# Zero rows of the last batch shared out by the engines' counted rows, the copies of the first two batches queued in another order, and one semaphore for the free transfers, in an argmax, gather and scatter kernel

## The chip, the core and the metric

The kernel runs on one core of one Trainium2 chip. The metric is device time in microseconds (us) of one execution. Executions of one kernel on one chip mostly agree within about 0.4%. The chips differ too: the kernel before took 857.7 us on one, 860.0 to 860.2 us on two others. So times are compared with the kernel before on the same chip in the same rounds.

## The reference

For each of 8 batches there are 2048 rows of 2048 scores, and 2048 value rows of 2560 float32 (10,240 bytes each). For each score row the reference finds the column of the largest score. It then adds that column's value row into the output at the same index, so an output row is its value row times the number of score rows that chose it.

```python
best_j = np.argmax(scores, axis=2)
gathered = values[b_idx, best_j, :].copy()
out = np.zeros_like(values)
np.add.at(out, (b_idx, best_j, slice(None)), gathered)
```

With the fixed inputs, of the 16,384 output rows 6,131 are chosen by nobody (they must be zero), 5,875 once (a copy of the value row) and 4,378 more than once (a scaled copy).

## The kernel before

(HBM stands for the memory of the source's DRAM tensors, the inputs and the output; its tiles are in SBUF, or in PSUM where their pool says so.) SyncE loads score tiles of 2 MB. VectorE finds each row's maximum and its index; TensorE adds one-hot matrices into a count for every column. From the counts VectorE makes index lists. GpSimd then issues indirect DMAs, 128 rows each: copies from HBM to HBM of the rows chosen once, zero rows from SBUF to HBM, and for the other rows a gather into SBUF (ScalarE scales them there) and a scatter. An index out of range skips its row: in the packet records it leaves a packet of 4 bytes, recorded as 9 ns, where a row that is moved is one of 10,240 bytes, 385 ns in the median. A copy needs only the counts, but a zero row or a gather needs the list, which is made later (cuts are marked):

```python
def value_steps(b, cnt_ps):
    # ... one_i: index of rows with count 1, out of range for the others
    first = NT if b == 0 else 4          # copies queued before the list exists (NT = 16)
    for t in range(first):
        copy_once(t)
    # ... ranks of the zero rows and of the others, by scans and two matmuls
    yield
    # ...
    oh = ohp.tile([P, 2 * NT, P], FP16)
    nc.vector.tensor_tensor(out=oh[:], in0=lo[:]..., in1=fill_f[:]..., op=ALU.is_equal)  # 4.4 us
    # ... matmuls that turn ranks into lists
    yield
    yield
    # ... zi, mi: the lists
    if b == 0:
        zeros()                          # 7 zero scatters
        for _ in range(10):
            yield
        gathers()                        # 5 gathers
    else:
        gathers()                        # each followed by one of the copies left over
        zeros()                          # likewise
    for k in range(MCAP):
        scatter(staged[k], mi[:, k:k + 1])
```

Each `yield` hands VectorE back to the scores of the next batch. For batch 0 the first four steps are taken at once, without pause. The transfers that nothing waits for (copies and zero rows) are "free": they increment `landed[b]`, one semaphore for each batch, and GpSimd waits for all eight at the end. `fill_f` decides on which partition of a list a rank falls; its order deals successive ranks out to the DMA engines in turn, if the map from partition to engine is the one that is read from the packets below.

## Time and profile before

| Kernel before | |
|---|---|
| median of 3 runs | 857.89 us (857.76 to 858.29) |
| span of the profiled run | 859.2 us |
| bytes moved by the DMA engines | 347.05 MB |
| rate in undisturbed slices | 427 GB/s |
| VectorE busy | 687.9 us, its last work at 708 us |
| last row packet ends | 847.4 us |

The page shows the span in 40 equal slices of 21.5 us, so slice 0 starts at 0 and slice 4 at 86 us. The first line is the busy share of the 16 DMA engines in tenths, the second what they moved.

```profile
DMA  9999899996999999999999999999999999999980
GB/s 378 427 427 427 289 390 428 419 413 248 428 419 426 427 426 429 426 429 424 427 426 428 425 427 428 429 426 425 428 424 420 424 426 413 425 425 421 425 370 35
DMA packets 47248, 347.05 MB, mean 404 GB/s; under 512 B 18278, under 2 KB 18278, under 8 KB 18278
```

The reader should see a kernel bound by its DMA engines: 427 GB/s nearly everywhere, and a few slices that fall short. Those are slices 4 and 5 (289 and 390), slice 9 (248) and the end (370 and 35). The windows view resolves them. Its columns are the stretch and its length, the busy time of each engine, TensorE's clock, the DMA engines' busy share, and GB/s.

```profile
core 0: us, PE busy (x) PEld busy (x) DVE busy (x) ACT busy (x) POOL busy (x), PEclk, DMA share, GB/s
86.00:116.00 30.00, 1.45 (x38) 1.40 (x38) 26.47 (x41) 0.00 (x0) 22.44 (x19) 1.00 0.89 308
186.00:208.00 22.00, 1.27 (x36) 1.19 (x36) 21.69 (x30) 0.00 (x0) 3.32 (x5) 1.00 0.65 240
830.00:838.00 8.00, 0.00 (x0) 0.00 (x0) 0.00 (x0) 0.00 (x0) 0.00 (x0) 1.00 0.64 269
838.00:848.00 10.00, 0.00 (x0) 0.00 (x0) 0.00 (x0) 0.00 (x0) 0.00 (x0) 1.00 0.17 69
848.00:859.10 11.10, 0.00 (x0) 0.00 (x0) 0.00 (x0) 0.00 (x0) 0.00 (x0) 1.00 0.00 0
```

From 830 us on no compute engine works; engines run out of rows one after the other (0.64, then 0.17 busy), and for the last 11 us no row moves. The timeline shows who should have fed slices 4 and 9. Its columns are start, duration, engine and line, operation, and in brackets the idle time before it and what ended it.

```profile
89.44 4.42 DVE L239 TENSOR_TENSOR oh<-lo,fill_f 128x4096 f16<-128x4096 uint32 x1
89.50 5.22 POOL L33 DMA_INDIRECT out_dram<-in_values_dram,ones_i  x1 [0.30 <-issue]
...
95.02 1.01 POOL L33 DMA_INDIRECT out_dram<-in_values_dram,ones_i  x1 [0.30 <-issue]
...
```

```profile
182.61 0.98 POOL L33 DMA_INDIRECT out_dram<-in_values_dram,ones_i  x1 [11.48 <-DVE m L214]
...
186.45 0.97 POOL L33 DMA_INDIRECT out_dram<-in_values_dram,ones_i  x1 [0.30 <-issue]
205.19 1.04 POOL L134 DMA_INDIRECT vbig<-in_values_dram,many_i  x1 [17.77 <-DVE empty L270]
```

In batch 0 one issue takes 5.22 us where the median of all 264 is 0.98 us. In batch 1 four copies are issued by 187.4 us, and then GpSimd waits 17.77 us for the list.

The *shortfall* of a stretch is its length less the time that the bytes moved in it would take at 427 GB/s, from the packet records, a packet's bytes spread over its duration. The *tail* is the time from an even end to the last row packet; the even end is 800 us plus a sixteenth of the time of all packets that start after 800 us. *After the last packet* is what remains of the span. In this trace the shortfall of 86 to 230 us is 18.9 us, the tail 10.2 us, and 11.7 us follow the last packet.

### The profile page before, as it was taken

To read this page: it belongs to the slowest core of one execution; us is meant where nothing else is said; L and a number is where in the kernel's file an instruction comes from. 1 tells how busy PE (TensorE), PEld (TensorE's weight loads), DVE (VectorE), ACT (ScalarE), POOL (GpSimd) and SP (SyncE) were. 2 spreads that over 40 slices of the span, in tenths; PEclk is the share of its full clock that TensorE was granted. 3 is DMA by queue.
4 is the path that set the end of the run, shared out by engine and by line. 5 is a ranking of instruction groups with operands and counts; after the bars stand their busy time and mean duration, and the time that the engine had idled before them with its cause. 6 is when DMAs were issued, how large, how long until landed. Compare 5 with 4: busy or idle time off the path is not lost.

```text
span 859.2 us, 2246 instructions
## 1 busy us (share of the span) xinstructions
PE 18.0 (2%) x400; PEld 17.0 (2%) x400; DVE 687.9 (80%) x741; ACT 103.2 (12%) x43; POOL 271.7 (32%) x275
## 2 busy tenths in 40 slices
PE   0000000000000000000000000000000000000000
PEld 0000000000000000000000000000000000000000
DVE  6999899999999999999999999999999980000000
ACT  2000000500320000220002300013100500500400
POOL 0000751213721027140056210451306715716500
DMA  9999899996999999999999999999999999999980
GB/s 378 427 427 427 289 390 428 419 413 248 428 419 426 427 426 429 426 429 424 427 426 428 425 427 428 429 426 425 428 424 420 424 426 413 425 425 421 425 370 35
DMA packets 47248, 347.05 MB, mean 404 GB/s; under 512 B 18278, under 2 KB 18278, under 8 KB 18278
## 3 DMA queue, kind: packets, MB, share of 16 engines
q0 software_dynamic: 38016, 212.67, 59.8%
q1 hardware_dynamic: 9216, 134.22, 37.1%
q14 instruction: 13, 0.11, 0.0%
q8 instruction: 3, 0.05, 0.0%
HBM read 354.42 MB, written 293.60 MB: 754 GB/s over the span
## 4 chain that ended last, share of the span: by engine, by line
DVE 69%; DMA 9%; POOL 7%; issue 5%; another core or an unknown queue 4%; PE 0%; POOLq 0%
DVE am L169 31%; DVE mx L168 29%; DMA out_dram<-vbig,many_i 8%; DVE oh L239 3%; POOL out_dram L33 3%; POOL out_dram L139 3%; DVE oh_lo L178 2%; POOL vbig L134 1%; DMA vbig<-in_scores_dram 1%; DVE lo L174 1%; DVE oh_hi L182 0%; DVE rz L247 0%; DVE hi L176 0%; DVE ez L243 0%
## 5 line engine op out<-in xcount | busy, mean ns | idle before, releaser
L169 DVE FIND_INDEX8 am<-mx,s_tile 128x8 uint32<-128x2048 f32 x116 | 265.1, 2285 | 0.0
L168 DVE MAX8 mx<-s_tile 128x8 f32<-128x2048 f32 x116 | 264.4, 2279 | 0.0
L280 ACT ACTIVATE vbig<-vbig,many_c 128x2560 f32<-128x2560 f32 x40 | 96.9, 2427 | 705.9 <-DMA vbig<-in_values_dram,many_i 703.1
L33 POOL DMA_INDIRECT out_dram<-in_values_dram,ones_i x128 | 130.1, 1016 | 155.3 <-DVE m L214 117.0
L134 POOL DMA_INDIRECT vbig<-in_values_dram,many_i x40 | 40.6, 1015 | 260.5 <-DMA out_dram<-vbig,many_i 198.1
L139 POOL DMA_INDIRECT out_dram<-vbig,many_i x40 | 41.4, 1035 | 105.8 <-ACT vbig L280 101.1
L139 POOL DMA_INDIRECT out_dram<-zrow,zero_i x56 | 58.3, 1042 | 17.1 <-issue 17.1
L239 DVE TENSOR_TENSOR oh<-lo,fill_f 128x4096 f16<-128x4096 uint32 x8 | 35.5, 4434 | 0.0
L168 DVE MAX8 mx<-vbig 128x8 f32<-128x2048 f32 x12 | 27.4, 2280 | 6.2 <-DMA vbig<-in_scores_dram 6.2
L169 DVE FIND_INDEX8 am<-mx,vbig 128x8 uint32<-128x2048 f32 x12 | 27.4, 2285 | 0.0
L178 DVE TENSOR_TENSOR oh_lo<-lo,lane_f 128x512 bf16<-128x512 uint32 x32 | 22.2, 695 | 0.3
L187 PE MATMUL cnt_ps<-oh_hi,oh_lo 128*128 128x16 bf16 x128 | 8.2, 174 | 571.2 <-DVE oh_hi L182 542.4
L187 PEld LDWEIGHTS <-oh_lo 128*128 128x128 bf16 x128 | 8.4, 105 | 570.9 <-DVE oh_lo L178 521.3
L169 DVE MATCH_VALUE_LOAD am<-mx,s_tile 128x8 f32 x116 | 10.7, 92 | 4.0
L174 DVE TENSOR_SCALAR lo<-am 128x4 uint32<-128x4 uint32 x32 | 6.1, 192 | 1.1
L182 DVE TENSOR_TENSOR oh_hi<-hi,lane_f 128x64 bf16<-128x64 uint32 x32 | 7.0, 218 | 0.0
L258 PE MATMUL m_ps<-rm,oh 128*128 128x16 f16 x128 | 4.7, 175 | 81.1 <-DVE rm L254 81.1
L176 DVE TENSOR_SCALAR hi<-am 128x4 uint32<-128x4 uint32 x32 | 6.1, 191 | 0.0
L258 PEld LDWEIGHTS <-oh 128*128 128x128 f16 x128 | 4.1, 105 | 81.6 <-DVE rm L254 74.8
L261 PE MATMUL z_ps<-rz,oh 128*128 128x16 f16 x128 | 4.6, 174 | 0.0
L261 PEld LDWEIGHTS <-oh 128*128 128x128 f16 x128 | 4.0, 104 | 0.0
L247 DVE TENSOR_TENSOR rz<-ez,row_f 128x256 f16<-128x256 f16 x8 | 3.4, 424 | 0.3
(52 smaller groups left out, 54.5 us busy)
## 6 DMA issues: line engine op xcount, KB each, us to landing
s_tile<-in_scores_dram SPq DMA_DIRECT2D x58, 2048.0 KB, 12.3
vbig<-in_scores_dram SPq DMA_DIRECT2D x6, 2048.0 KB, 19.1
out_dram<-in_values_dram,ones_i POOLq DMA_INDIRECT x128
out_dram<-zrow,zero_i POOLq DMA_INDIRECT x56
vbig<-in_values_dram,many_i POOLq DMA_INDIRECT x40
out_dram<-vbig,many_i POOLq DMA_INDIRECT x40
```

The source lines that it names most:

```text
L33: return eng.add_instruction(ins)
L134: nc.gpsimd.indirect_dma_start(out=v, out_offset=None, in_=values_flat[:, :], in_offset=bass.IndirectOffsetOnAxis(ap=idx, axis=0), bounds_ ...
L139: note(nc.gpsimd.indirect_dma_start(out=out_flat[:, :], out_offset=bass.IndirectOffsetOnAxis(ap=idx, axis=0), in_=v, in_offset=None, bound ...
L168: nc.vector.max(out=mx[:], in_=rows)
L169: nc.vector.max_index(out=am[:, g, :], in_max=mx[:], in_values=rows)
L174: nc.vector.tensor_single_scalar(out=lo[:], in_=am[:, :, 0], scalar=P - 1, op=ALU.bitwise_and)
L178: nc.vector.tensor_tensor(out=oh_lo[:], in0=lo[:].unsqueeze(2).to_broadcast([P, G, P]), in1=lane_f[:].unsqueeze(1).to_broadcast([P, G, P]) ...
L187: nc.tensor.matmul(out=cnt_ps[:], lhsT=oh_lo[:, g, :], rhs=oh_hi[:, g, :], start=(t == 0), stop=(t == NT - 1))
L239: nc.vector.tensor_tensor(out=oh[:], in0=lo[:].unsqueeze(2).to_broadcast([P, 2 * NT, P]), in1=fill_f[:].unsqueeze(1).to_broadcast([P, 2 * ...
L258: nc.tensor.matmul(out=m_ps[:], lhsT=oh[:, NT + t, :], rhs=rm[:, t, :, :].rearrange("p a k -> p (a k)"), start=(t == 0), stop=(t == NT - 1))
L261: nc.tensor.matmul(out=z_ps[:], lhsT=oh[:, t, :], rhs=rz[:, t, :], start=(t == 0), stop=(t == NT - 1))
L280: nc.scalar.activation(out=v, in_=v, func=mybir.ActivationFunctionType.Copy, bias=0.0, scale=mc[:, k:k + 1])
```

## The change

The intent has three parts. (1) Each engine's rows are counted, and the zero rows of the last batch are shared out so that all engines get equal totals. Twelve zero scatters instead of seven carry the uneven shares, and `fill_f` gets a new order in which rank r goes to engine r mod 16 by the same map. (2) Batch 0 queues 6 copies instead of 16 and then zero rows and copies in turn; batch 1 queues all 16 copies, instead of 4, before its list exists. (3) One semaphore serves all free transfers. The diff, cut to its core:

```diff
-    landed = [tc.alloc_semaphore(f"landed{b}") for b in range(B)]
+    landed = tc.alloc_semaphore("landed")
...
+    def level_engines(rank, lo, hi):
+        # copies: rows with count 1, of partitions 8 e to 8 e + 7, for engine e
+        # share: (total + 15 - e) // 16 rows of each list
+        ... work = copies + zeros of batches 0 to 6 + 2 * (rows chosen more than once)
+        ... more = min(max(work) - work, CORR); quota = more + even
+        ... hi = nth >> 3; lo = (nth & 7) * 16 + eng
...
+        nc.vector.tensor_tensor(out=notone[:], in0=notone[:], in1=one_b[:], op=ALU.add)
...
-        first = NT if b == 0 else 4
+        first = (6, NT)[b] if b < 2 else 4
...
+        if b == B - 1:
+            level_engines(rank[:, 0, :], lo[:, 0:NT], hi[:, 0, :])
...
-            for k in range(ZCAP):
+            for k in range(ZLAST if b == B - 1 else ZCAP):
...
-    for b in range(B):
-        nc.gpsimd.wait_ge(landed[b], 16 * n_free[b])
+    nc.gpsimd.wait_ge(landed, 16 * n_free[0])
```

More of the change, by code (lines that the diff above doesn't have):

```diff
@@ L55 @@
     NM = NT // 2
+    NE = 16
+    LE = P // NE
     ZCAP, MCAP = 7, 5
+    ZLAST = 12
+    CORR = 56
     values_flat = values.rearrange("b s h -> (b s) h")
@@ L66 @@
     ohp = ctx.enter_context(tc.tile_pool(name="ohp", bufs=1))
+    lev = ctx.enter_context(tc.tile_pool(name="lev", bufs=1))
     lists = ctx.enter_context(tc.tile_pool(name="lists", bufs=1))
@@ L77 @@
     fill_i = consts.tile([P, P], INT32)
-    for a in range(4):
-        first, step = (a >> 1) + 8 * (a & 1) + 16 * (a & 1), 16 - 32 * (a & 1)
-        nc.gpsimd.iota(fill_i[:, a * 32:(a + 1) * 32].rearrange("p (x y z) -> p x y z", x=4, y=2),
-                       pattern=[[2, 4], [step, 2], [32, 4]], base=first, channel_multiplier=0)
+    nc.gpsimd.iota(fill_i[:].rearrange("p (a b c d) -> p a b c d", a=2, b=2, c=NE // 2),
+                   pattern=[[NE // 2, 2], [4 * NE, 2], [1, NE // 2], [NE, 4]], base=0, channel_multiplier=0)
     part_i = consts.tile([P, 1], INT32)
@@ L99 @@
     nc.vector.memset(ones_f[:], 1.0)
-    totmax = consts.tile([P, 2], FP32)
-    nc.vector.memset(totmax[:], 0.0)
+    part8_i = consts.tile([P, 1], INT32)
+    nc.vector.tensor_single_scalar(out=part8_i[:], in_=part_i[:], scalar=3, op=ALU.logical_shift_right)
+    part8_f = consts.tile([P, 1], FP32)
+    nc.vector.tensor_copy(part8_f[:], part8_i[:])
+    rowset = consts.tile([P, NE], FP32)
+    nc.vector.tensor_scalar(out=rowset[:], in0=lane_f[:, 0:NE], scalar1=part8_f[:, 0:1], scalar2=None, op0=ALU.is_equal)
+    up_f = consts.tile([P, NE], FP32)
+    nc.vector.tensor_scalar(out=up_f[:], in0=lane_f[:, 0:NE], scalar1=-1.0, scalar2=NE - 1.0, op0=ALU.mult, op1=ALU.add)
+    tots = consts.tile([P, 2, B], FP32)
+    most = consts.tile([P, 1], FP32)
+    notone = consts.tile([P, NT], FP32)
+    nc.vector.memset(notone[:], 0.0)
     zero1 = consts.tile([P, 1], FP32)
@@ L119, in writes_out, with free_running @@
         tc.add_to_no_dep_group("out", ins.ins)
-    landed = [tc.alloc_semaphore(f"landed{b}") for b in range(B)]
-    n_free = [0] * B
-    def free_running(b):
-        def note(ins):
-            writes_out(ins)
-            ins.then_inc(landed[b], 16)
-            tc.info.no_tile_sem_insts.add(ins.ins.name)
-            n_free[b] += 1
-        return note
+    landed = tc.alloc_semaphore("landed")
+    n_free = [0]
+    def free_running(ins):
+        writes_out(ins)
+        ins.then_inc(landed, 16)
+        tc.info.no_tile_sem_insts.add(ins.ins.name)
+        n_free[0] += 1
     def gather(v, idx):
@@ L189, in count_steps @@
                 yield
+    def level_engines(rank, lo, hi):
+        X = mybir.AxisListType.X
+        row = lev.tile([P, 1], FP32)
+        nc.vector.tensor_reduce(out=row[:], in_=notone[:], op=ALU.add, axis=X)
+        nc.vector.tensor_scalar(out=row[:], in0=row[:], scalar1=-1.0 / BIG, scalar2=float(B * NT), op0=ALU.mult, op1=ALU.add)
+        rows = lev.tile([P, NE], BF16)
+        nc.vector.tensor_scalar(out=rows[:], in0=rowset[:], scalar1=row[:, 0:1], scalar2=None, op0=ALU.mult)
+        copies = psum_f.tile([P, NE], FP32)
+        nc.tensor.matmul(out=copies[:], lhsT=ones[:], rhs=rows[:], start=True, stop=True)
+        share = lev.tile([P, NE, 2 * B], INT32)
+        nc.vector.tensor_tensor(
+            out=share[:], in0=tots[:].rearrange("p c b -> p (c b)").unsqueeze(1).to_broadcast([P, NE, 2 * B]),
+            in1=up_f[:].unsqueeze(2).to_broadcast([P, NE, 2 * B]), op=ALU.add)
+        nc.vector.tensor_single_scalar(out=share[:], in_=share[:], scalar=4, op=ALU.logical_shift_right)
+        load = lev.tile([P, 2, NE], FP32)
+        nc.vector.tensor_reduce(out=load[:, 0, :], in_=share[:, :, 0:B - 1], op=ALU.add, axis=X)
+        nc.vector.tensor_reduce(out=load[:, 1, :], in_=share[:, :, B:2 * B], op=ALU.add, axis=X)
+        work = lev.tile([P, NE], FP32)
+        nc.vector.scalar_tensor_tensor(out=work[:], in0=load[:, 1, :], scalar=2.0, in1=load[:, 0, :], op0=ALU.mult, op1=ALU.add)
+        nc.vector.tensor_tensor(out=work[:], in0=work[:], in1=copies[:], op=ALU.add)
+        top = lev.tile([P, 1], FP32)
+        nc.vector.tensor_reduce(out=top[:], in_=work[:], op=ALU.max, axis=X)
+        more = lev.tile([P, NE], FP32)
+        nc.vector.tensor_scalar(out=more[:], in0=work[:], scalar1=-1.0, scalar2=top[:, 0:1], op0=ALU.mult, op1=ALU.add)
+        zeros = tots[:, 0, B - 1:B]
+        fits = lev.tile([P, 1], FP32)
+        nc.vector.tensor_single_scalar(out=fits[:], in_=zeros, scalar=float(NE * (NT * LE - CORR)), op=ALU.is_le)
+        nc.vector.tensor_scalar(out=more[:], in0=more[:], scalar1=float(CORR), scalar2=fits[:, 0:1], op0=ALU.min, op1=ALU.mult)
+        all_more = lev.tile([P, 1], FP32)
+        nc.vector.tensor_reduce(out=all_more[:], in_=more[:], op=ALU.add, axis=X)
+        even = lev.tile([P, 1], FP32)
+        nc.vector.tensor_tensor(out=even[:], in0=zeros, in1=all_more[:], op=ALU.subtract)
+        even_i = lev.tile([P, 1], INT32)
+        nc.vector.tensor_scalar(out=even_i[:], in0=even[:], scalar1=NE - 1.0, scalar2=0.0, op0=ALU.add, op1=ALU.max)
+        nc.vector.tensor_single_scalar(out=even_i[:], in_=even_i[:], scalar=4, op=ALU.logical_shift_right)
+        nc.vector.tensor_copy(even[:], even_i[:])
+        quota = lev.tile([P, NE], FP32)
+        nc.vector.tensor_scalar(out=quota[:], in0=more[:], scalar1=even[:, 0:1], scalar2=None, op0=ALU.add)
+        nc.vector.tensor_reduce(out=most[:], in_=quota[:], op=ALU.max, axis=X)
+        ends = lev.tile([P, NE], FP32)
+        nc.vector.tensor_tensor_scan(out=ends[:], data0=ones_f[:, 0:NE], data1=quota[:], initial=0.0, op0=ALU.mult, op1=ALU.add)
+        past = lev.tile([P, NT, NE], FP32)
+        nc.vector.tensor_tensor(
+            out=past[:], in0=rank.unsqueeze(2).to_broadcast([P, NT, NE]),
+            in1=ends[:].unsqueeze(1).to_broadcast([P, NT, NE]), op=ALU.is_ge)
+        eng = lev.tile([P, NT], FP32)
+        nc.vector.tensor_reduce(out=eng[:], in_=past[:], op=ALU.add, axis=X)
+        nc.vector.tensor_tensor(out=past[:], in0=past[:], in1=quota[:].unsqueeze(1).to_broadcast([P, NT, NE]), op=ALU.mult)
+        begin = lev.tile([P, NT], FP32)
+        nc.vector.tensor_reduce(out=begin[:], in_=past[:], op=ALU.add, axis=X)
+        nth = lev.tile([P, NT], U32)
+        nc.vector.tensor_tensor(out=nth[:], in0=rank, in1=begin[:], op=ALU.subtract)
+        nc.vector.tensor_single_scalar(out=hi, in_=nth[:], scalar=3, op=ALU.logical_shift_right)
+        lane = lev.tile([P, NT], U32)
+        nc.vector.tensor_single_scalar(out=lane[:], in_=nth[:], scalar=LE - 1, op=ALU.bitwise_and)
+        nc.vector.scalar_tensor_tensor(out=lo, in0=lane[:], scalar=float(NE), in1=eng[:], op0=ALU.mult, op1=ALU.add)
@@ L201, in value_steps @@
         nc.vector.tensor_copy(one_i, one_f[:])
+        nc.vector.tensor_tensor(out=notone[:], in0=notone[:], in1=one_b[:], op=ALU.add)
         def copy_once(t):
-            free_running(b)(scatter_rows_in_dram(
+            free_running(scatter_rows_in_dram(
                 nc, out_flat[:, :], values[b, t * P:(t + 1) * P, :], one_i[:, t:t + 1], last_row))
-        first = NT if b == 0 else 4
+        first = (6, NT)[b] if b < 2 else 4
         for t in range(first):
@@ L229, in value_steps @@
         yield
-        nc.vector.tensor_tensor(out=totmax[:], in0=totmax[:], in1=tot_ps[:], op=ALU.max)
-        rank = fin.tile([P, 2, NT], U32)
+        nc.vector.tensor_copy(tots[:, :, b], tot_ps[:])
+        rank = fin.tile([P, 2, NT], FP32)
         for c in range(2):
             nc.vector.tensor_scalar(out=rank[:, c, :], in0=base[:, c, :], scalar1=off_ps[:, c:c + 1], scalar2=None, op0=ALU.add)
+        place = fin.tile([P, 2, NT], U32)
+        nc.vector.tensor_copy(place[:], rank[:])
         lo = fin.tile([P, 2 * NT], U32)
-        nc.vector.tensor_single_scalar(out=lo[:], in_=rank[:].rearrange("p c t -> p (c t)"), scalar=P - 1, op=ALU.bitwise_and)
+        nc.vector.tensor_single_scalar(out=lo[:], in_=place[:].rearrange("p c t -> p (c t)"), scalar=P - 1, op=ALU.bitwise_and)
         hi = fin.tile([P, 2, NT], U32)
-        nc.vector.tensor_single_scalar(out=hi[:], in_=rank[:], scalar=7, op=ALU.logical_shift_right)
+        nc.vector.tensor_single_scalar(out=hi[:], in_=place[:], scalar=7, op=ALU.logical_shift_right)
+        if b == B - 1:
+            level_engines(rank[:, 0, :], lo[:, 0:NT], hi[:, 0, :])
         oh = ohp.tile([P, 2 * NT, P], FP16)
@@ L286, in zeros @@
         def zeros():
-            for k in range(ZCAP):
-                scatter(zrow[:], zi[:, k:k + 1], free_running(b))
+            for k in range(ZLAST if b == B - 1 else ZCAP):
+                scatter(zrow[:], zi[:, k:k + 1], free_running)
                 if rest:
@@ L320 @@
             pass
-        over = fin.tile([1, 2], FP32)
-        nc.vector.tensor_single_scalar(out=over[:, 0:1], in_=totmax[0:1, 0:1], scalar=float(ZCAP * P), op=ALU.is_gt)
-        nc.vector.tensor_single_scalar(out=over[:, 1:2], in_=totmax[0:1, 1:2], scalar=float(MCAP * P), op=ALU.is_gt)
+        full = fin.tile([1, 2], FP32)
+        nc.vector.tensor_reduce(out=full[:, 0:1], in_=tots[0:1, 0, 0:B - 1], op=ALU.max, axis=mybir.AxisListType.X)
+        nc.vector.tensor_reduce(out=full[:, 1:2], in_=tots[0:1, 1, :], op=ALU.max, axis=mybir.AxisListType.X)
+        over = fin.tile([1, 3], FP32)
+        nc.vector.tensor_single_scalar(out=over[:, 0:1], in_=full[:, 0:1], scalar=float(ZCAP * P), op=ALU.is_gt)
+        nc.vector.tensor_single_scalar(out=over[:, 1:2], in_=full[:, 1:2], scalar=float(MCAP * P), op=ALU.is_gt)
+        nc.vector.tensor_single_scalar(out=over[:, 2:3], in_=most[0:1, :], scalar=float(ZLAST * LE), op=ALU.is_gt)
         over_i = fin.tile([1, 1], INT32)
-        nc.vector.tensor_tensor(out=over_i[:], in0=over[:, 0:1], in1=over[:, 1:2], op=ALU.add)
-    for b in range(B):
-        nc.gpsimd.wait_ge(landed[b], 16 * n_free[b])
+        nc.vector.tensor_reduce(out=over_i[:], in_=over[:], op=ALU.max, axis=mybir.AxisListType.X)
+    nc.gpsimd.wait_ge(landed, 16 * n_free[0])
     more = nc.values_load(over_i[0:1, 0:1], engines=[mybir.EngineType.Pool], min_val=0, max_val=2)
@@ L331 @@
         for b in range(B):
-            for k in range(ZCAP, NT):
+            for k in range(ZLAST if b == B - 1 else ZCAP, NT):
                 scatter(zrow[:], zero_i[:, b * NT + k:b * NT + k + 1])
```

## The prediction

> **What bounds it now.** The DMA engines. The page's slices show 420 to 430 GB/s almost everywhere; 347 MB at 427 GB/s are 813 of the 859 us. VectorE is busy 688 us, but ends at 708 us (timeline); later only DMA counts. In the packet records a 10,240 byte row costs one engine 385 ns where it is not starved. Time is lost only where engines idle, in three places:
>
> 1. Slices 4 and 5 (86 to 116 us): 290 and 390 GB/s. Copies of batch 0 are issued one per 1.28 us (timeline); one carries about 45 used rows, so GpSimd feeds only about 360 GB/s. Shortfall against 427: about 8 us.
> 2. Slice 9 (186 to 208 us): 248 GB/s. Four copies of batch 1 are issued by 187.4, then GpSimd waits 17.8 us for the list (waits: the gather after VectorE's empty). Shortfall: 9.6 us.
> 3. The tail: the windows view gives DMA share 0.57 for 830 to 840 us, 0.11 for 840 to 850. The last packet ends at 847.4; the same work shared evenly would end at about 837. Some 11 us follow the last landing (drains, semaphore reset), untouched by the change.
>
> I counted rows per engine from the fixed inputs[...] and assuming eight consecutive rows per engine for copies from HBM to HBM. No view shows a packet's engine, so the map is not confirmed; the total, 20,762 rows, equals the trace's 10,240 byte packets. Before: 1,266 to 1,320 rows an engine, the heaviest 22 over the mean, 8.6 us. The records show about 10.5 us, so some 2 us come from something else than rows.
>
> **What the change does.**
> - Levelling: with the new quotas I count 1,299 at most, mean 1,297.6. Gain: 10.5 us less the 2 us that rows do not explain, about 8.2.
> - Batch 1 queues 16 copies at once: twelve more, 5.5 MB, 13 us of DMA work, issued between 187 and 203 us, where slice 9 idles. With the score loads that is over 427 GB/s on average; about 1 us of shortfall remains.
> - Batch 0 issues 6 copies, then zeros and copies in turn: about 1.6 MB per 2.56 us, over 600 GB/s, from about 100 us. The shortfall from 100 to 116 us (3 us) goes; that of 86 to 100 us (5 us, with one issue of 5.2 us) stays. The earlier finish is kept only because batch 1's copies fill what follows. Places 1 and 2 together: about 11 us.
> - Added: five scatters, 640 skipped rows of 9 ns over 16 engines (0.4 us); some 35 small VectorE operations near 700 us (about 8 us), off the path; 0.4 us of VectorE per batch.
> - One semaphore for eight: nothing.
>
> **Prediction.** 857.9 - 11 - 8.2 + 0.4 = 839.1 us, range 834.5 to 844. Chances: faster by over 2% (under 840.7) 0.64, within 2% 0.35, slower 0.01.
>
> **What would show it.** Slice 9 at 400 GB/s or more; slice 5 near 420, slice 4 still low; full rate until about 827 us, then an end within 3 us instead of 17; last VectorE work around 715 us; bytes unchanged.
>
> **What would make it wrong.** A wrong engine map: the tail stays 10 us or grows. Backlog spent early: a new gap before batch 1's copies (175 to 182 us) or in batch 2 (275 to 295 us), giving back several us. Engines slower for reasons other than rows would leave more tail.

The map was an assumption, and the row counts of each engine, with the 8.2 us that use them, were the estimate from it; the packets of the runs show the map (see "The engines, told apart by their packets").

## The result

| | before | changed |
|---|---|---|
| median | 858.09 us (4 runs) | 845.36 us (845.06 to 845.43, 4 runs) |
| ratio | | 0.9849 (0.9832 to 0.9866) |
| shortfall, 86 to 230 us | 18.9 us | 11.2 us |
| tail | 10.2 us | 5.9 us |
| after the last packet | 11.7 us | 8.7 us |

The changed kernel is 1.5% faster, 12.7 us by the medians. The prediction was 839.1 us and its range ended at 844.0 us: the time is outside it. Of its chances, "within 2%" (0.35) came about. Repeated in other rounds the ratio was 0.986 (0.9843 to 0.9876), 845.43 against 857.67 us. The three rows above sum to 15.0 us, more than 12.7. The trace of before is of an execution of 860.97 us, 2.9 us over its median, and the two profiled spans differ by 15.6 us, so a sum over two traces is good to about 3 us.

The slices of the changed kernel's page:

```profile
DMA  9999899999999999999999999999999999999992
GB/s 376 430 428 428 308 414 420 426 395 375 426 428 427 426 428 428 426 425 427 431 425 425 428 427 427 424 429 428 426 429 420 426 424 414 422 423 423 424 417 121
DMA packets 47968, 347.05 MB, mean 411 GB/s; under 512 B 18998, under 2 KB 18998, under 8 KB 18998
```

Slice 9 rose from 248 to 375 GB/s but not to 400; slice 8 fell from 413 to 395; slice 4 is still low. The bytes are the same. The windows that answer to those of before:

```profile
86.00:116.00 30.00, 1.45 (x38) 1.40 (x38) 28.38 (x46) 0.00 (x0) 22.05 (x20) 1.00 0.92 338
182.00:208.00 26.00, 1.28 (x36) 1.19 (x36) 25.59 (x33) 0.00 (x0) 21.02 (x17) 1.00 0.98 366
818.00:826.00 8.00, 0.00 (x0) 0.00 (x0) 0.00 (x0) 0.00 (x0) 0.00 (x0) 1.00 0.92 384
826.00:835.00 9.00, 0.00 (x0) 0.00 (x0) 0.00 (x0) 0.00 (x0) 0.00 (x0) 1.00 0.36 150
835.00:843.50 8.50, 0.00 (x0) 0.00 (x0) 0.00 (x0) 0.00 (x0) 0.00 (x0) 1.00 0.00 0
```

In 182 to 208 us the engines are 0.98 busy and yet move only 366 GB/s: some packets last longer there (of the rows that started in that stretch the mean took 434 ns and a tenth over 490, against a mean of 385 in 300 to 600 us), so the busy share hides part of the shortfall. Starved stretches show the same: of the rows that started in 95 to 100 us of the kernel before, the median took 385 ns and a tenth over 950 ns. The end is still staggered, 0.92 and then 0.36 busy. The program now ends 8.7 us after the last packet. The timeline of the new copies of batch 1:

```profile
185.93 0.97 POOL L33 DMA_INDIRECT out_dram<-in_values_dram,ones_i  x1 [0.30 <-issue]
...
187.16 4.43 DVE L316 TENSOR_TENSOR oh<-lo,fill_f 128x4096 f16<-128x4096 uint32 x1
187.21 5.22 POOL L33 DMA_INDIRECT out_dram<-in_values_dram,ones_i  x1 [0.31 <-issue]
...
192.74 1.02 POOL L33 DMA_INDIRECT out_dram<-in_values_dram,ones_i  x1 [0.30 <-issue]
...
204.56 0.97 POOL L33 DMA_INDIRECT out_dram<-in_values_dram,ones_i  x1 [0.31 <-issue]
205.84 1.03 POOL L146 DMA_INDIRECT vbig<-in_values_dram,many_i  x1 [0.30 <-issue]
```

The copies continue past 187 us as intended, but now one of them stands for 5.22 us beside VectorE's comparison, as one did in batch 0 before.

### The profile page after: what moved, and what is told of

It reads as the page before. It is cut to its first block, busy times and chain, and to the rows that moved or that the text cites. A ratio compares the mean times of both kernels' runs of the same rounds, so it can differ in the third digit from the quotient of the medians.

```text
span 843.6 us, 2305 instructions
## 1 busy us (share of the span) xinstructions
PE 18.1 (2%) x401; PEld 17.0 (2%) x401; DVE 696.7 (83%) x793; ACT 103.0 (12%) x43; POOL 286.5 (34%) x277
## 2 busy tenths in 40 slices
DMA packets 47968, 347.05 MB, mean 411 GB/s; under 512 B 18998, under 2 KB 18998, under 8 KB 18998
## 4 chain that ended last, share of the span: by engine, by line
DVE 68%; DMA 9%; POOL 8%; issue 6%; another core or an unknown queue 5%; PE 0%; POOLq 0%
DVE am L181 30%; DVE mx L180 28%; DMA out_dram<-vbig,many_i 8%; DVE oh L316 3%; POOL out_dram L151 3%; POOL out_dram L33 3%; DVE oh_lo L190 2%; POOL vbig L146 1%; DMA vbig<-in_scores_dram 1%; DVE lo L186 1%; DVE oh_hi L194 0%; DVE rz L324 0%; DVE ez L320 0%; DVE hi L188 0%
## 5 line engine op out<-in xcount | busy, mean ns | idle before, releaser
L33 POOL DMA_INDIRECT out_dram<-in_values_dram,ones_i x128 | 133.9, 1046 | 145.8 <-DVE m L287 107.7
L146 POOL DMA_INDIRECT vbig<-in_values_dram,many_i x40 | 46.8, 1169 | 231.9 <-DMA out_dram<-vbig,many_i 182.1
L151 POOL DMA_INDIRECT out_dram<-vbig,many_i x40 | 44.9, 1122 | 123.1 <-ACT vbig L357 118.6
L151 POOL DMA_INDIRECT out_dram<-zrow,zero_i x61 | 59.8, 981 | 18.9 <-issue 18.3
```

Source lines behind the costliest of these rows:

```text
L33: return eng.add_instruction(ins)
L146: nc.gpsimd.indirect_dma_start(out=v, out_offset=None, in_=values_flat[:, :], in_offset=bass.IndirectOffsetOnAxis(ap=idx, axis=0), bounds_ ...
L151: note(nc.gpsimd.indirect_dma_start(out=out_flat[:, :], out_offset=bass.IndirectOffsetOnAxis(ap=idx, axis=0), in_=v, in_offset=None, bound ...
```

## The engines, told apart by their packets

No view names a packet's engine. But each engine should see its own sequence of used rows (10,240 bytes) and skipped rows (4 bytes), and this sequence follows from the inputs and the map from partition to engine. Near the end only GpSimd's queue is active, and an engine's next packet starts 2 to 5 ns before the recorded end of the one before. Following packets back from the end by this rule, each of the 16 predicted sequences was found, for 100 packets at least and often for over 900, before the match broke. In most runs the sixteen matches ended on sixteen different packets. A wrong packet can match for some 120 packets, as the last lists are alike, so an end found by a match that broke so early is less sure. In e5 and e9 engine 2 shares its packet with another engine: its end there is not settled (its lag in the regrouped run below included). The long matches cover copies as well as lists, so the assumed map holds in these traces: partition p of a list, for zero rows, gathers and scatters, belongs to engine 8 (p div 64) + (p div 4) mod 8, and in copies from HBM to HBM engine e takes rows 8 e to 8 e + 7. Counted once more on the trace of the result, with one more packet of 4 bytes an engine after each DMA (the page's 18,998 packets under 512 B are 13,670 skipped rows and 16 for each of 333 DMAs), the sixteen matches are 247 to 1,010 packets long, fifteen of them over 540. With partitions 8 e to 8 e + 7 taken for the lists too, no match passes 37 packets; with the lists' map taken for the copies too, none passes 106.

The matches give each engine's end. The *lag* is that end with 0.38 us for each row over or under the mean taken off, less the mean over engines: what rows do not explain. *Early copies* are the used rows of the 16 copies of batch 0 and the first four of batch 1. "Regrouped" is the run e9_regrouped below. "Before" and "changed" are the traces of the kernels as they were run again with the experiments.

| engine | rows, before | end, before | rows, changed | end, changed | lag, changed | early copies, changed | lag, regrouped | early copies, regrouped |
|---|---|---|---|---|---|---|---|---|
| 0 | 1320 | 843.7 | 1299 | 827.1 | -1.9 | 55 | -0.8 | 53 |
| 1 | 1317 | 838.2 | 1299 | 824.4 | -4.6 | 68 | +1.6 | 56 |
| 2 | 1306 | 834.2 | 1299 | 824.9 | -4.1 | 73 | +1.6 | 55 |
| 3 | 1319 | 846.3 | 1299 | 829.4 | +0.5 | 57 | +0.6 | 63 |
| 4 | 1304 | 844.3 | 1299 | 832.1 | +3.2 | 49 | +5.3 | 47 |
| 5 | 1283 | 831.0 | 1299 | 828.6 | -0.3 | 53 | -0.5 | 53 |
| 6 | 1284 | 830.7 | 1299 | 825.9 | -3.1 | 64 | -2.1 | 61 |
| 7 | 1291 | 835.0 | 1299 | 831.7 | +2.7 | 49 | -0.2 | 56 |
| 8 | 1294 | 839.6 | 1299 | 832.0 | +3.0 | 44 | -4.7 | 64 |
| 9 | 1272 | 829.6 | 1298 | 833.2 | +4.7 | 50 | -4.5 | 63 |
| 10 | 1320 | 841.6 | 1299 | 823.7 | -5.2 | 64 | +4.6 | 52 |
| 11 | 1288 | 832.6 | 1299 | 830.7 | +1.8 | 59 | -3.4 | 66 |
| 12 | 1270 | 832.7 | 1293 | 834.7 | +8.0 | 43 | -0.2 | 56 |
| 13 | 1306 | 836.3 | 1299 | 827.0 | -1.9 | 66 | +0.1 | 60 |
| 14 | 1291 | 832.1 | 1299 | 828.4 | -0.5 | 63 | +1.4 | 53 |
| 15 | 1297 | 832.6 | 1284 | 821.1 | -2.2 | 62 | +1.3 | 60 |

The levelling does what it says: 1,299 rows on nearly every engine. Still the engines end from 821 to 835 us. The lag falls by 0.36 us for each early copy row (correlation -0.87). That suggested a theory. While the engines starve, they wait for the next copy to be issued, so a row that moves then costs its engine nothing: it would otherwise have idled. The levelling counts such rows as work and gives their engine too few zero rows. One rival is that some engines are slow by themselves. Another is that every copy row is cheaper than other rows; then the later copies would count as much as the early ones.

## The experiments

"Shortfall" is that of 86 to 230 us unless a stretch is named.

| run | edit | median us | before, same rounds | ratio | shortfall | tail | after last |
|---|---|---|---|---|---|---|---|
| after_again | none | 845.43 | 857.67 | 0.9860 | 10.8 | 5.9 | 8.7 |
| before_again | none, kernel before | 859.83 (1 run) | 860.15 | | 18.6 | 9.6 | 11.7 |
| e1_level_only | copies queued as before | 855.25 | 860.00 | 0.9943 | 19.4 | 6.0 | 8.7 |
| e2_queue_only | no levelling | 851.64 | 860.00 | 0.9896 | 12.4 | 11.6 | 8.7 |
| e3_count_less | early copies not counted | 843.09 | 860.00 | 0.9803 | 12.5 | 2.6 | 8.7 |
| e4_fill_psum | comparison's input in PSUM | 844.23 | 860.00 | 0.9817 | 10.4 | 5.1 | 8.7 |
| e5_reversed | batches 7 to 0 | 842.63 | 857.67 | 0.9827 | 9.4 | 4.3 | 8.7 |
| e6_early_list | list of batch 1 at once | 846.83 | 857.67 | 0.9875 | 11.6 | 6.6 | 8.7 |
| e7_early_psum | e6 and e4 | 843.50 | 860.15 | 0.9806 | 9.4 | 5.7 | 8.7 |
| e8_eight_sems | eight semaphores | 849.05 | 857.67 | 0.9900 | 10.8 | 5.2 | 12.2 |
| e9_regrouped | other rows in each copy | 847.05 | 860.15 | 0.9846 | 12.6 | 5.2 | 8.9 |
| e10_all_three | e6, e4 and e3 | 840.88 | 860.15 | 0.9774 | 9.3 | 2.4 | 8.7 |
| e11_before_one_sem | kernel before, one semaphore | 856.72 | 860.06 | 0.9960 | 18.7 | 9.4 | 8.3 |
| e12_four_sems | four semaphores | 847.88 | 860.06 | 0.9863 | 12.6 | 5.8 | 9.0 |

Each run has one profile, of one of its executions; e2's took 853.6 us, 2.0 over its median. All gave the right result.

### The two kernels again

Both were run again beside the others, unedited.

> The changed kernel as it is, on the chip of this call, so that the other three can be compared with it directly. Every theory: 0.985 of the kernel before.

> The kernel before, once more, for a trace from the chip of these runs: last packet at about 847, tail about 10 us, shortfall of 86 to 230 us about 19 us. Since eight semaphores in the changed kernel lengthened what follows the last packet from 8.7 to 12.2 us, here too 11.7 us or so must follow the last packet.

Both came out as expected. The 11.7 us after the last packet of the kernel before are there again, so they were not an accident of one profile.

### Each half alone: e1_level_only and e2_queue_only

```diff
 e1: -        first = (6, NT)[b] if b < 2 else 4
     +        first = NT if b == 0 else 4
 e2: -    CORR = 56
     +    CORR = 0
```

> The changed kernel with the copies queued as before (16 in batch 0, 4 in batch 1): the levelling alone. All theories: the shortfalls of 86 to 116 us (8.5 us) and 182 to 208 us (9.7 us) stay as before. If the engines' lag that rows do not explain is the one seen before (up to 7.2 us over the mean), the tail (last packet against an even end) shrinks only from 10.2 to about 7 us: time 855.3 us, gain 2.6. If the levelling worked in full it would be 848.

> The changed kernel with the correction limited to 0 rows, so that every engine gets an even share of the last batch's zero rows: the queueing alone. Shortfalls as in the changed kernel (6.4 us in 86 to 116 us, 3.7 us in 182 to 208 us), tail back to about 10.9 us: time about 850.5 us, 5 us over the changed kernel. If levelling does nothing after all: 845.4.

e1 gained 4.8 us by the medians where 2.6 were expected, e2 8.4 us where about 7 were. The shortfalls behaved as expected: e1 keeps that of before, e2 has about that of the changed kernel. The tails were 6.0 and 11.6 us, against 7 and 10.9. Both runs have one semaphore, and the gain of that (see the runs on semaphores) was missing from both expectations. With e11's 0.9960 divided out, levelling alone is 0.9983 (about 1.5 us) and queueing alone 0.9936 (about 5.5 us). Their product with e11 is 0.988, less of a gain than the changed kernel's 0.985 to 0.986. By these numbers the halves help each other by about 2 us, and the tails agree: with the new queueing an unlevelled end is worse (11.6 us) than in the kernel before (9.6). But each ratio is known to about 0.0013 only, the runs of e2 spread from 849.0 to 853.9 us, and the 11.6 us are of one of its slower executions, so this is not shown.

A smaller tail is also not all gain. In e1 the tail is 3.6 us shorter than in before_again, but the last row packet comes only 1.5 us earlier (844.7 against 846.2), because the even end came 2 us later. Of these, 0.8 us are shortfall in 86 to 230 us, and 0.9 us in 690 to 760 us, the stretch in which the last batch's list is now made later; some 0.4 us are the added skipped rows (an estimate: 640 packets of 9 ns over 16 engines).

### Which rows to count: e3_count_less

```diff
-        nc.vector.tensor_tensor(out=notone[:], in0=notone[:], in1=one_b[:], op=ALU.add)
+        lead = (NT, 4)[b] if b < 2 else 0
+        if lead < NT:
+            nc.vector.tensor_tensor(out=notone[:, lead:], in0=notone[:, lead:], in1=one_b[:, lead:], op=ALU.add)
```

The constant that turns this sum into a count is lessened by the same 20 columns.

> The changed kernel, with the copies of batch 0 and the first four copies of batch 1 left out of the count that the levelling evens (they move while GpSimd's issues, not the engines, set the pace). Supply theory (a row moved while the engines are starved costs its engine nothing): tail 5.9 -> 2.9 us, time 842.4 us. If the lag that remains is scatter from run to run, or comes from anything not tied to these rows, the tail stays at 6 us or grows: 845 or more. A theory of engines slow by themselves gives the same as the supply theory here only if the lag happens to follow these rows; the run with reversed batches tells these two apart.

```profile
817.00:825.00 8.00, 0.00 (x0) 0.00 (x0) 0.00 (x0) 0.00 (x0) 0.00 (x0) 1.00 1.02 424
825.00:833.00 8.00, 0.00 (x0) 0.00 (x0) 0.00 (x0) 0.00 (x0) 0.00 (x0) 1.00 0.56 235
833.00:841.30 8.30, 0.00 (x0) 0.00 (x0) 0.00 (x0) 0.00 (x0) 0.00 (x0) 1.00 0.00 0
```

The engines are now full to 825 us and stop together within the next 7.5 us; the tail is 2.6 us against 2.9 expected. The ratio is 0.9803, clear of both measurements of the changed kernel. The rows are now less equal (1,284 to 1,314 an engine) and the end is more even. The lag that remained came back with the same pattern (correlation 0.98 with the repeat of the changed kernel), so it is not scatter from run to run. As the expectation said, this run does not tell the two theories apart.

### Engine or rows: e5_reversed and e9_regrouped

```diff
 e5: scores[b, ...] -> scores[B - 1 - b, ...]; values and row offsets likewise
 e9: -    nc.gpsimd.iota(row_i[:], pattern=[[P, NT]], base=0, channel_multiplier=1)
     +    nc.gpsimd.iota(row_i[:], pattern=[[1, NT]], base=0, channel_multiplier=NT)
     (index split into index >> 4 and index & 15 instead of & 127 and >> 7)
     -   values[b, t * P:(t + 1) * P, :]
     +   values[b].rearrange("(p t) h -> t p h", t=NT)[t]
```

> The changed kernel taking the batches in the order 7 to 0; same work, same levelling rule. The end of each engine is read from the packet records. Speed theory (an engine lags by itself): the lags keep their engines: engine 12 last (5.9 us over the mean), 9 and 8 next, 1 and 10 first (5.5 us under); tail 5.9 us. Supply theory (rows that moved while the engines were starved cost nothing; the lag follows the copies of the first two batches in order): the lags now follow the copy rows of batches 7 and 6; they do not correlate with those of the changed kernel (computed correlation -0.15), engine 2 or 6 is about the last, 7 or 10 the first, and the tail is 3.2 to 3.6 us.

> The changed kernel with copy t of a batch taking the rows 16 p + t instead of 128 t + p: same rows, but engine e now copies rows 128 e to 128 e + 127, so the copy rows of each engine are drawn anew; the levelling counts them as before. Engine theory (the lag that rows do not explain belongs to the engine): the lags stay those of the changed kernel, engine 12 (8 us over the mean) last, 10 and 1 first, correlation with them near 1, tail 8.2 us. Supply theory (it belongs to the copy rows that moved while engines were starved): the lags correlate with the new early copy rows at about -0.37 us a row and not with the old lags (computed correlation -0.17); engine 4 about last (4 us), 3, 11 and 15 first, tail about 4 us. A correlation with the old lags between 0.3 and 0.7 would mean both.

e5 did not decide it. Its lags correlate with those of the changed kernel by 0.66 (0.69 with the first trace), where the supply theory had -0.15 and the engine theory 1. Engine 12 was again late (5.4 us), though the tail was smaller, 4.3 us. With the new early copy rows they correlate by -0.39 (-0.21 us a row), but that hangs on engine 2, whose end is not settled: without it the figures are -0.61 and -0.36 us a row, and 0.64 with the old lags. The early rows also differ less between engines than before (standard deviation 5.0 rows, against 8.6 for batches 0 and 1), so this was a weak test.

e9 decided it. Its lags correlate with the new early copy rows by -0.78, at -0.42 us a row, and with the old lags by -0.39. The last columns of the table above show it engine by engine: engine 12 goes from 8.0 to -0.2, engine 9 from 4.7 to -4.5, engine 10 from -5.2 to 4.6. (Without engine 2 the three figures are -0.78, -0.41 and -0.36.) Engine 4, expected about last, is last. Other details of the expectation missed: of the engines expected first only 11 was among them, after 8 and 9, and the tail was 5.2 us where about 4 was expected. The theory of engines slow by themselves falls. So, in this run, does that of cheaper copies: fitted together, an early copy row counts -0.43 us and a later one +0.02 us (-0.37 and -0.07 in the repeat of the changed kernel). The slope is about the time of one row, 0.385 us, as it must be if the engine would otherwise have idled for that time. What is left of the lag, with a standard deviation of some 1.7 us after the early rows, was not explained. Part of it may be where "early" was cut off: with the first 12 copies of batch 1 counted instead of 4, which in the changed kernel moved in the short stretch of 182 to 208 us too, the correlation in e9 is -0.91. That was tried after the fact. What kept engine 12 late in e5 stays open; there the lags follow all copy rows of an engine best (correlation -0.80, -0.14 us a row), so in that run a share of later copies is not excluded.

### The long issue: e4_fill_psum

```diff
+    fill_p = psum_f.tile([P, P], FP32)
+    nc.vector.tensor_copy(fill_p[:], fill_f[:])
...
-            in1=fill_f[:].unsqueeze(1).to_broadcast([P, 2 * NT, P]), op=ALU.is_equal)
+            in1=fill_p[:].unsqueeze(1).to_broadcast([P, 2 * NT, P]), op=ALU.is_equal)
```

In the trace of the changed kernel each of the six issues that began beside a comparison took 3.4 to 5.2 us, where the median issue takes 0.98 us. The comparison reads two inputs from SBUF; that this is what holds the issue up was the theory, and this run moves one of the two to PSUM.

> The changed kernel, with the second input of the 4.43 us comparison that builds oh read from PSUM instead of SBUF. Lock theory (GpSimd's issue cannot go on while VectorE runs an operation with two SBUF inputs): no issue longer than 1.5 us overlaps an oh any more (in the changed kernel six of eight do, 3.4 to 5.2 us each); the shortfall of 86 to 100 us falls from 4.7 to about 2, that of 182 to 208 us from 3.7 to about 1: time about 841. Rival[...]: the long issues stay, time 845.4.

The same place in e4's timeline:

```profile
186.78 4.42 DVE L318 TENSOR_TENSOR oh<-lo,fill_p 128x4096 f16<-128x4096 uint32 x1
186.83 0.97 POOL L33 DMA_INDIRECT out_dram<-in_values_dram,ones_i  x1 [0.31 <-issue]
188.11 0.97 POOL L33 DMA_INDIRECT out_dram<-in_values_dram,ones_i  x1 [0.30 <-issue]
189.39 0.97 POOL L33 DMA_INDIRECT out_dram<-in_values_dram,ones_i  x1 [0.31 <-issue]
190.66 0.97 POOL L33 DMA_INDIRECT out_dram<-in_values_dram,ones_i  x1 [0.30 <-issue]
```

The comparison takes 4.42 us as before, and four issues of 0.97 us pass beside it. In the whole run no issue that overlaps a comparison exceeds 1.1 us. So it is the second input in SBUF that makes the stall here: only that input was edited, and the issues fell from 3.4 to 5.2 us to 1.1 us at most. In the changed kernel the long issues ended about 0.85 us after the comparison did, in all six cases. The other order shows no block: two issues that began 0.25 and 0.76 us before a comparison took 0.99 and 0.98 us, and the comparison 4.42 us as always. Nor was every issue held up that began second: in the kernel before one that began 0.04 us after a comparison took 0.98 us, and that comparison 4.50 us. Now the shortfalls, e4 first and then the changed kernel:

```profile
86.00:100.00 14.00, 1.45 (x38) 1.40 (x38) 12.51 (x34) 0.00 (x0) 8.17 (x8) 1.00 0.95 354
182.00:208.00 26.00, 1.27 (x36) 1.19 (x36) 25.62 (x33) 0.00 (x0) 17.78 (x19) 1.00 0.98 360
```

```profile
86.00:100.00 14.00, 1.45 (x38) 1.40 (x38) 12.51 (x34) 0.00 (x0) 10.01 (x7) 1.00 0.82 288
```

86 to 100 us went from 288 to 354 GB/s: its shortfall fell from 4.7 to 2.5 us, near the 2 expected. But 182 to 208 us stayed at 360 GB/s, a shortfall of 4.3 us where 1 was expected. There the lock theory's second half failed: the stall is real, but it alone does not make that shortfall. Against e3, which has the long issues and ran on the same chip in the same rounds, the shortfall of 86 to 230 us fell from 12.5 to 10.4 us, and that is just what 86 to 100 us gained (4.5 to 2.5). The ratio, 0.9817, lies below both of the changed kernel's, by about 3 us.

### Work known earlier: e6_early_list and e7_early_psum

```diff
-        first = (6, NT)[b] if b < 2 else 4
+        first = 6 if b < 2 else 4
...
-        yield            (the three before the lists)
+        if b != 1:
+            yield
```

> The changed kernel, with the lists of batch 1 made without pause, as those of batch 0 are, and 6 copies before them instead of 16, the other ten between the gathers and zero rows. Theory of missing work (until about 208 us the shortfall is set by how much work has been made known, not by how fast GpSimd issues it): lists known at about 194 instead of 205 us bring the shortfall of 182 to 208 us from 3.7 down to about 2, the part before 190 us staying; time 1 to 2 us under the changed kernel. Rival (the issue stall under oh makes the shortfall): it stays at 3.7 or grows, since the stall is still there.

> The early list of batch 1 together with the comparison's input in PSUM. With the early list alone the shortfall of 182 to 208 us was 5.4 us, 4.6 of them before 196 us, where a 4.4 us issue stood under oh; from 196 on it was gone. If both causes are real (work not known in time, and the issue stall when nothing else is queued), both together bring 182 to 208 us to about 2.5 us, less than either alone (4.3 and 5.4): time 2 us under the changed kernel, about 843.5. If the stall did not matter, 5.4 us stay and the time is that of the early list alone, 846.8.

The two halves of the stretch, for the repeat of the changed kernel, for e6 and for e7:

```profile
182.00:196.00 14.00, 1.02 (x32) 0.93 (x32) 13.79 (x18) 0.00 (x0) 11.72 (x8) 1.00 0.95 356
196.00:208.00 12.00, 0.25 (x4) 0.26 (x4) 11.80 (x16) 0.00 (x0) 9.14 (x9) 1.00 1.01 362
```

```profile
182.00:196.00 14.00, 1.02 (x32) 0.93 (x32) 13.08 (x17) 0.00 (x0) 11.56 (x9) 1.00 0.80 276
196.00:208.00 12.00, 0.25 (x4) 0.26 (x4) 11.86 (x13) 2.43 (x1) 9.26 (x10) 1.00 1.00 418
```

```profile
182.00:196.00 14.00, 1.02 (x32) 0.93 (x32) 12.92 (x17) 0.00 (x0) 9.76 (x10) 1.00 0.93 331
196.00:208.00 12.00, 0.26 (x4) 0.26 (x4) 11.86 (x13) 2.43 (x1) 9.22 (x9) 1.00 1.01 426
```

e6 was 1.4 us slower than the changed kernel, and the shortfall of 182 to 208 us grew to 5.4 us, as the rival had it and not the theory. But its two halves part: from 196 us on the rate rose from 362 to 418 GB/s, while before 196 us it fell from 356 to 276 (5.0 us short; the 4.6 in e7's expectation is too low). There the long issue now met a moment when nothing else was queued:

```profile
182.12 4.43 DVE L317 TENSOR_TENSOR oh<-lo,fill_f 128x4096 f16<-128x4096 uint32 x1
...
183.02 4.37 POOL L33 DMA_INDIRECT out_dram<-in_values_dram,ones_i  x1 [0.30 <-issue]
```

With both edits the early half recovers to 331 GB/s and the late half is full, 426 GB/s. The time, 843.50 us, was as expected; the shortfall of 182 to 208 us is 3.3 us, less than with either edit alone but over the 2.5 expected.

The packet records say where those 3.3 us are. From 187 to 196 us of e7 the score queue moves nothing at all, and what GpSimd has issued (copies, from 189.7 us on gathers too) brings about 350 GB/s. In the changed kernel's repeat the score queue moves 0.10 MB in 184 to 187 us, of the 1.28 MB that 427 GB/s would be, and nothing from 196 to 205 us. There too the copies are alone, at about 370 GB/s. Part of that may be slower rows: in e4, from 200 to 204 us, when all copies had been issued and nearly 16 engines were copying from HBM to HBM, one row took 467 and 480 ns (medians) instead of 385. From 196 to 199 us of the same run, with as many engines copying, the median row still took 385 ns. Why, no run here settles.

### One semaphore: e8_eight_sems, e11_before_one_sem and e12_four_sems

```diff
 e8:  -    landed = tc.alloc_semaphore("landed")
      +    landed = [tc.alloc_semaphore(f"landed{b}") for b in range(B)]   (the waits too)
 e11: the opposite edit, in the kernel before
 e12: four, one for two batches
```

> The changed kernel with eight semaphores for the free transfers instead of one: within 0.5 us of the changed kernel in every theory.

> The kernel before, with one semaphore for the free transfers instead of eight and nothing else. If the number of semaphores sets the closing part of the program: what follows the last packet falls from 11.7 to 8.7 us, shortfall and tail stay (18.6 and 9.6 us), time 3.0 us under the kernel before, ratio 0.9965. If it came from something else in the changed kernel: no change.

> The changed kernel with four semaphores for the free transfers. If each costs the same: 0.5 us for each of three more, so 10.2 us after the last packet instead of 8.7 (one) and 12.2 (eight), and 1.5 us over the changed kernel (about 846.9 where that takes 845.4). If the cost is a step and not a slope: 8.7 or 12.2 us.

The expectation for e8 was wrong, and in an instructive way: eight semaphores cost the changed kernel 3.6 us (849.05 against 845.43 on the same chip). The windows from the last packet on, e8 first and then e11:

```profile
835.20:847.20 12.00, 0.00 (x0) 0.00 (x0) 0.00 (x0) 0.00 (x0) 0.00 (x0) 1.00 0.00 0
```

```profile
846.30:854.40 8.10, 0.00 (x0) 0.00 (x0) 0.00 (x0) 0.00 (x0) 0.00 (x0) 1.00 0.00 0
```

In e8 12.2 us pass after the last packet, in the changed kernel 8.7. e11 shows that nothing else of the change is needed: one semaphore in the kernel before takes 3.3 us off, at a ratio of 0.9960, and what follows the last packet falls from 11.7 to 8.3 us while shortfall and tail stay. In the instruction records the closing drain of GpSimd is 8.98 us with eight semaphores in e8 and 6.12 us with one in the changed kernel; the semaphore instruction before it takes 1.89 and 1.34 us (in the trace of the kernel before the two take 8.57 and 1.84 us). The edits also change the number of GpSimd's waits, eight or one, but these cost nothing after the last packet: that instruction starts 0.5 us after the last row packet in both. e12 had four and was expected to lie between. Its profiled run has 9.0 us, much like one semaphore, but its runs spread from 846.3 to 849.2 us, and the profiled one is the fastest. Its ratio, 0.9863, is little over the changed kernel's (0.9849 and 0.9860). Whether the cost is a step or a slope stays open.

### All together: e10_all_three

> The same, and the copies of batch 0 and the first four of batch 1 left out of the levelled count. If the effects add, the tail falls by another 3 us, to about 3: time about 840.5 us, the fastest of all.

("The same" is the kernel of e7.)

```profile
182.00:208.00 26.00, 1.27 (x36) 1.19 (x36) 24.76 (x29) 3.32 (x2) 18.96 (x19) 1.00 0.96 373
814.00:822.00 8.00, 0.00 (x0) 0.00 (x0) 0.00 (x0) 0.00 (x0) 0.00 (x0) 1.00 1.01 419
822.00:830.00 8.00, 0.00 (x0) 0.00 (x0) 0.00 (x0) 0.00 (x0) 0.00 (x0) 1.00 0.62 259
```

The edits add: against e7, in the same rounds, the tail fell by 3.3 us and the time by 2.6 us. The engines are full to 822 us, the tail is 2.4 us, and the kernel takes 840.88 us, a ratio of 0.9774 (0.9761 to 0.9788). It beats both kernels: 2.3% against before, and about 0.8% against the changed kernel by the ratios.

## Why the prediction was wrong

Its sum was 857.9 - 11 - 8.2 + 0.4 = 839.1 us. Term by term:

- **What bounds the kernel** was right. Apart from the semaphores, only the filling of DMA time moved the time, and the bytes are the same. The last VectorE work ended at 716 us, as predicted (715). Whether the added work there costs something is open: the shortfall of 690 to 760 us is 0.8 to 1.0 us in the two traces of the kernel before and in e11's, and 0.4 to 1.9 us in the others.
- **The engine map** was right, and is now confirmed by packet sequences (247 to 1,010 packets an engine in the trace of the result). (The least loaded engine has 1,270 rows in the table, not 1,266.)
- **"Levelling: ... about 8.2" is the step that failed most.** The tail fell by 4.3 us (10.2 to 5.9; 3.7 in the repeats). The prediction took the difference between 10.5 and 8.6 us as "some 2 us [that] come from something else than rows". That subtracted the maxima of two unlike distributions. In truth the lag that rows do not explain ran from -5.4 to +6.9 us over the engines of the kernel before (before_again), and partly cancelled the row imbalance: engine 12 had the fewest rows (1,270) and the largest lag. Levelling the rows laid the lag bare. The lag follows copy rows that moved while the engines starved (e9), and leaving these out of the count gives a tail of 2.6 us (e3).
- **"Places 1 and 2 together: about 11 us"** measured 7.7 (18.9 to 11.2), 7.8 in the repeats. The mis-sized part is "about 1 us of shortfall remains" in place 2: 3.7 us remained, 4.2 in the repeat. The step used an average, "with the score loads that is over 427 GB/s on average", but the two supplies did not coincide. The score queue was emptied while GpSimd stood in a long issue, and was then silent for 9 us while the copies came alone. Work known earlier filled the half after 196 us (e6: 362 to 418 GB/s), and without the stall the half before it was still short (e7: 331 GB/s). The prediction also assumed 1.28 us for each new issue, though the trace of before already showed a 5.22 us issue beside the comparison. The new copies of batch 1 were moved beside the next one. In place 1 the shortfall from 100 to 116 us fell from 3.3 to 1.7 us and was not wholly gone. That 86 to 100 us would stay was right.
- **"One semaphore for eight: nothing"** was wrong by about 3.3 us (e11), in the other direction. Without this unforeseen gain the miss would have been larger.
- **"Added: ... 0.4 us"** was too small to be seen apart. (The added VectorE operations near 700 us run from 700.8 to 707.9 us, 7.1 us where about 8 were predicted.)
- Of the named dangers, none came true as named: no gap appeared before batch 1's copies (0.1 us of shortfall in 160 to 182 us) or in batch 2 (0.1 us in 270 to 300 us). "Engines slower for reasons other than rows would leave more tail" came nearest: the tail did stay, but the engines are not slower.

With the measured sizes the sum is 857.9 - 7.7 - 4.3 - 3.3 + 0.4 = 843 us, 2.4 us under the measured 845.4. That is within the 3 us by which the profiled execution of before was over its median.

## What to carry to other kernels

When engines share work that comes in bursts, level their end times and not their counts: a unit of work that ran while its engine would have idled was free here (-0.43 us of lag an early row in e9, where a row takes 0.385 us), and counting it cost about 3 us of tail (e3). Before queueing more indirect DMAs at some place, look at what VectorE runs there, since here a comparison of 4.43 us with two SBUF inputs held up all six issues that began beside it in the changed kernel, for 3.4 to 5.2 us each, and reading one input from PSUM took the stall away (no issue over 1.1 us beside it in e4). Do not average two supplies over a stretch; ask for each moment whether one alone is enough. And try the small part of a change by itself: the one costed at nothing here was worth 3.3 us.
